# Rounded weights by a casting DMA on Pool's queue instead of copies on ACT, in a hybrid attention block on one core

## The chip, the cores and the metric

The kernel runs as one program on one core of a Trainium2 chip. A core has a matrix engine (TensorE, PE in the profile, with its weight loads shown apart as PEld), a vector engine (DVE), an activation engine (ACT), a general engine (GpSimd, POOL) and a queue engine (SP) that here only issues DMAs. Every engine works through its own list of instructions in order and waits on semaphores for the others. Sixteen DMA engines move data between the main memory and the core's buffer memory; a DMA is issued from the queue of SP, ACT or POOL.

The metric is the device time of one execution in microseconds, the median of three runs.

## The reference

The reference is a decoder block for 512 tokens of width 1024, in float32, with 16 meta tokens put in front (528 rows):

```
h = layer_norm(concat(meta, x))
proj = h @ w_in                       # w_in is 1024 x 10240: ten projections of 1024 columns
q_d,k_d,v_d,g_d, q_s,k_s,v_s,g_s, m_d,m_s = split(proj)
y_d = softmax attention with ALiBi, 8 heads of two 64-wide halves: p0 - lam * p1, then RMS norm per head
y_s = stick-breaking attention, 16 heads of 64 (a reversed running product of sigmoids)
br_d = (y_d * silu(g_d)) @ w_br_diff ;  br_s = (y_s * silu(g_s)) @ w_br_sb
merged = sigmoid(m_d + b0) * br_d + sigmoid(m_s + b1) * br_s
out = layer_norm(2**0.25 * h + merged @ w_out)[16:]
```

## The kernel before

**Products in three parts.** The matrix engine is fed with a rounded 32-bit type (`F32R`). To keep float32 accuracy every operand is split into a rounded part and the rest: `hTh` and `hTl` hold the normalised input, transposed, and each weight tile `raw` becomes `wh` (rounded) and `wl = raw - wh`. A product is then three matmuls: `wh` with `hTh`, `wh` with `hTl`, `wl` with `hTh`.

**Weights.** A weight is a block of 128 output columns, loaded as a tile of 128 partitions x 8 x 128 (512 KB). The list `seq` holds 96 of them in the order in which they are used: 80 blocks of `w_in` and 8 each of the two branch matrices. Weight number n has three tiles, `raw`, `wh` and `wl`, and each kind has three buffers in rotation. `load` (L83) issues the loads of `raw` on SP's queue, `hi` (L91) makes `wh` by a copy on ACT (L97), half a tile at a time, and `lo` (L99) makes `wl` by a subtraction on DVE (L103), half a tile at a time. `prep(n, half)` (L105) calls the three of them; it is called by the projection two places earlier, once when it starts and once half way.

**Projections.** `proj_tok` (L350) is one block for the 512 tokens: 8 slices of three matmuls of 128x512 (L356, L357, L358), 24 in all. `proj_pos` (L363) is one block for all 528 rows, as two halves of 264: 48 matmuls (L370).

**Stages.** After a start (normalisation, the first two query blocks, the first key and value blocks) come 16 units: eight heads of the softmax branch ("d") and eight pairs of heads of the stick-breaking branch ("s"). While the scores of one unit are worked out, the projections of the next are woven in: three weights per d unit (key, value, query), five per s unit (two gates more). Scores are matmuls (L495, L501) whose results DVE and ACT work on (L508, L579, L583, L589, L590 for d; L639, L642, L643, L645, L646 for s); PE then turns them (L514, L519), ACT and DVE split them (L524, L525), and PE multiplies them with the values. POOL does small parts: the ALiBi bias of a head (L563), the low part of the squares (L612), the gating of a result (L388). The late stage (from L720) makes the two branch products and the merge gates, 128x512 projections one after another, and POOL adds the two branches (L740); a tail multiplies with `w_out` and normalises.

**Order.** The statements are not run in the order of the code. From the start on, the framework's scheduler places every instruction on its engine by a timeline of its own, so a change in what an instruction is or where it runs moves the others. The chip then keeps that order on each engine: an instruction that waits holds everything behind it on its engine.

Of the kernel before, what the change touches and what calls it, by code (L numbers as in the profile page):

```python
# [10 lines left out]
F32R = mybir.dt.float32r  # L11
# [5 lines left out]
P = 128  # L17
D = 1024
KT = D // P
# [13 lines left out]
COL = dict(qd=0, kd=1024, vd=2048, gd=3072, qs=4096, ks=5120, vs=6144, gs=7168, md=8192, ms=9216)  # L33
# [10 lines left out]
def hybrid_block_kernel(ctx: ExitStack, tc: tile.TileContext, x, meta, emb_g, emb_b, w_in, b_gate,  # L44
                        diff_lambda, subln_g, w_br_d, w_br_s, w_out, ln_g, ln_b, out):
    nc = tc.nc
    v, s, g, pe = nc.vector, nc.scalar, nc.gpsimd, nc.tensor

    w_in = w_in[0].rearrange("(k p) n -> p k n", p=P)
    w_br_d = w_br_d[0].rearrange("(k p) n -> p k n", p=P)  # L50
    w_br_s = w_br_s[0].rearrange("(k p) n -> p k n", p=P)
# [4 lines left out]
    wpool = ctx.enter_context(tc.tile_pool(name="w", bufs=3))  # L56
# [11 lines left out]
    seq = [("qd", 0), ("qd", 1), ("kd", 0), ("vd", 0)]  # L68
# [11 lines left out]
    raws, split = [], []  # L80
    AHEAD = 2

    def load(n):  # L83
        while len(raws) < min(n, len(seq)):
            kind, i = seq[len(raws)]
            src, c = {"bd": (w_br_d, i * P), "bs": (w_br_s, i * P)}.get(kind) or (w_in, COL[kind] + i * P)
            raw = wpool.tile([P, KT, P], F32, tag="raw", name="raw", bufs=3)
            nc.sync.dma_start(raw, src[:, :, c:c + P])
            raws.append(raw)

    def hi(n, half):  # L91

        if half == 0:
            assert len(split) == n
            split.append([wpool.tile([P, KT, P], F32R, tag=w, name=w) for w in ("wh", "wl")])
        o = ts(half, 4)
        s.copy(split[n][0][:, o, :], raws[n][:, o, :])  # L97

    def lo(n, half, eng=v):  # L99

        o = ts(half, 4)
        wh, wl = split[n]
        eng.tensor_tensor(wl[:, o, :], raws[n][:, o, :], wh[:, o, :].bitcast(F32), op=ALU.subtract)  # L103

    def prep(n, half):  # L105

        load(n + 2)
        if n < len(seq):
            hi(n, half)
            lo(n, half)  # L110

    state = {"n": 0}

# [19 lines left out]
    for o in (ts(0, 512), ts(1, 512)):  # L133
        nc.sync.dma_start(xts[0][:, o], x[0, ts(0, P), o])
    nc.sync.dma_start(xts[1], x[0, ts(1, P), :])
    load(2)
    nc.sync.dma_start(xts[2], x[0, ts(2, P), :])
    nc.sync.dma_start(xts[3], x[0, ts(3, P), :])
    nc.sync.dma_start(mt, meta)
    load(3)  # L140
    nc.sync.dma_start(rows2[0:16], b_gate[0].rearrange("a (k p) -> (a k) p", p=P))
    nc.sync.dma_start(rows2[16:17], subln_g)
# [207 lines left out]
    def proj_tok(res, kind, i, hh=hTh, hl=hTl, o=M):  # L350
        n, wh, wl = weights(kind, i)
        ps = pj.tile([P, 512], F32, tag="pj", name="ps")
        for k in range(KT):
            if k == 0 or k == 4:
                prep(n + AHEAD, k // 4)
            pe.matmul(ps, wh[:, k, :], hh[:, k, o:], start=(k == 0), stop=False)  # L356
            pe.matmul(ps, wh[:, k, :], hl[:, k, o:], start=False, stop=False)  # L357
            pe.matmul(ps, wl[:, k, :], hh[:, k, o:], start=False, stop=(k == KT - 1))  # L358
            if k < KT - 1:
                yield 0.64  # L360
        res.append(ps)

    def proj_pos(res, kind, i):  # L363
        n, wh, wl = weights(kind, i)
        for c in range(2):
            ps = pj.tile([P, 512], F32, tag="pj", name="ps")
            prep(n + AHEAD, c)
            for k in range(KT):
                for m, (a, b) in enumerate(((wh, hTh), (wh, hTl), (wl, hTh))):
                    pe.matmul(ps[:, :H2], a[:, k, :], b[:, k, ts(c, H2)], start=(k == 0 and m == 0),  # L370
                              stop=(k == KT - 1 and m == 2))
                if k < KT - 1:
                    yield 0.33
            res.append(ps)
            if c == 0:
                yield 0.33
# [36 lines left out]
    with tc.tile_pool(name="att", bufs=1) as ap:  # L413
# [259 lines left out]
        for n in range(2):  # L673
            units[n]["A"] = A0[n]
        prep(3, 0)
        prep(3, 1)
        run(keys_values(units[0], *UNITS[0]))
# [82 lines left out]
    for c in range(2):  # L760
        for k in range(0, KT, 2):
            raw = wpool.tile([P, 2, 512], F32, tag="raw", name="rawo", bufs=3)
# [6 lines left out]
    for t in range(NB):  # L769
# [4 lines left out]
        for o, w in parts:  # L774
            c, r = o // 512, ds(o % 512, w)
            ps = pj.tile([P, 512], F32, tag="pj", name="pso")[:, :w]
            for k in range(KT):
                mh, ml = MH[:, k, ts(t, P)], ML[:, k, ts(t, P)]
                wh, wl = WO[c][0][:, k, r], WO[c][1][:, k, r]
# [4 lines left out]
            w = 256 if last else 512  # L784
# [55 lines left out]
```

## Time and profile before

| | |
|---|---|
| time, median of 3 runs | 752.0 us (751.91 to 752.81) |
| the profiled execution's own time | 751.83 us |
| its span, first to last instruction | 750.1 us |
| mean granted clock of the matrix engine | 0.993 |
| PE busy / weight loads busy | 733.0 us (98%) / 651.4 us (87%) |
| DVE busy | 543.7 us (72%) |
| ACT busy | 413.2 us (55%) |
| POOL busy | 85.2 us (11%) |
| moved by DMA | 63.90 MB, 85 GB/s in the mean |

The span is shorter than the time by 1.7 us, which lie before the first and after the last instruction. "Busy" for an engine means that some instruction of it is under way; a wait in front of an instruction is idle time, which the views put down to the instruction that ended it. The busy time of PE overlaps between neighbouring matmuls: a 128x512 matmul is shown with 393 ns, but the next one starts earlier than that. In the rows of a timeline the columns are the start, the duration, engine, line, operation, what is written and read, the shape, and in brackets the idle time before it with what ended it.

### The profile page before, as it was taken

Reading aid. Unit: us, or ns where it says so; the run is one execution under the profiler, and the core shown is the slowest. Engines: PE = TensorE matmul, PEld = TensorE weight load, DVE = VectorE, ACT = ScalarE, POOL = GpSimd, SP = SyncE. Lnnn points to the kernel's source line nnn. Section 1 sums busy time; section 2 is a strip of 40 time slices with the busy share of each in tenths; the row PEclk is TensorE's granted clock in tenths of the full one; section 3 lists DMA queues with packets and bytes.
Section 4 is the critical chain, followed back from the end, with each engine's and each line's share of the span. In section 5 each row is a group of like instructions: output and inputs, shape, how many; then the busy total and the mean of one; then the engine's idle time right before and its main releaser. Section 6 shows DMA issues by size and latency. Waiting matters only on the chain.

```text
span 750.1 us, 11849 instructions
## 1 busy us (share of the span) xinstructions
PE 733.0 (98%) x4390; PEld 651.4 (87%) x4390; DVE 543.7 (72%) x1181; ACT 413.2 (55%) x983; POOL 85.2 (11%) x106
## 2 busy tenths in 40 slices
PE   7999999999999999999999999999999999999996
PEld 6899999999999979898989898988878888888885
DVE  6888898888887789695969596967478343335555
ACT  6476777676777787575647474746473232324200
POOL 5510110111000000000000000001001000000101
PEclk8999999999999999999999999999999999999998
DMA  8132112121212121212222222122244333325221
GB/s 260 32 114 85 57 57 85 57 81 51 68 57 86 56 85 39 75 57 85 57 84 58 84 57 85 57 86 57 84 168 142 110 87 102 95 85 195 86 85 57
DMA packets 105340, 63.90 MB, mean 85 GB/s; under 512 B 2065, under 2 KB 100530, under 8 KB 105282
## 3 DMA queue, kind: packets, MB, share of 16 engines
q1 hardware_dynamic: 104098, 58.93, 26.6%
q10 hardware_dynamic: 1184, 4.20, 1.6%
q8 instruction: 35, 0.57, 0.3%
q14 instruction: 23, 0.19, 0.1%
HBM read 61.03 MB, written 2.10 MB: 84 GB/s over the span
## 4 chain that ended last, share of the span: by engine, by line
PE 90%; DVE 5%; ACT 3%; DMA 1%; issue 1%; POOL 0%; SPq 0%; DVEq 0%; ACTq 0%; POOLq 0%
PE ps L370 23%; PE ps L357 14%; PE ps L358 14%; PE ps L356 14%; PE sc L501 5%; PE t L514 3%; PE pso L782 2%; PE pso L781 2%; PE pso L780 2%; PE t L519 1%; PE av L659 1%; DMA raw<-in_w_in_dram 1%; PE tv L471 1%; PE av L655 1%; DVE hTl L239 1%
## 5 line engine op out<-in xcount | busy, mean ns | idle before, releaser
L103 DVE TENSOR_TENSOR wl<-raw,wh 128x512 fp32r<-128x512 f32 x187 | 131.5, 732 | 63.5 <-ACT wh L97 63.3
L97 ACT CAST wh<-raw 128x512 fp32r<-128x512 f32 x192 | 109.8, 621 | 120.8 <-PE ps L357 111.0
L370 PE MATMUL ps<-hTh,wh 128*128 128x264 f32 x512 | 147.5, 288 | 0.5 <-ACT k L452 0.4
L370 PE MATMUL ps<-hTl,wh 128*128 128x264 f32 x512 | 146.4, 286 | 0.0
L370 PE MATMUL ps<-hTh,wl 128*128 128x264 f32 x512 | 146.3, 286 | 0.0
L356 PE MATMUL ps<-hTh,wh 128*128 128x512 f32 x368 | 144.7, 393 | 0.0
L357 PE MATMUL ps<-hTl,wh 128*128 128x512 f32 x368 | 144.4, 392 | 0.0
L358 PE MATMUL ps<-hTh,wl 128*128 128x512 f32 x368 | 144.3, 393 | 0.0
L370 PEld LDWEIGHTS ps<-hTh,wh 128*128 128x128 f32 x512 | 96.5, 188 | 2.6 <-ACT k L452 0.9
L370 PEld LDWEIGHTS ps<-hTl,wh 128*128 128x128 f32 x512 | 96.6, 189 | 1.1
L370 PEld LDWEIGHTS ps<-hTh,wl 128*128 128x128 f32 x512 | 96.5, 188 | 0.0
L358 PEld LDWEIGHTS ps<-hTh,wl 128*128 128x128 f32 x368 | 69.1, 188 | 13.9
L357 PEld LDWEIGHTS ps<-hTl,wh 128*128 128x128 f32 x368 | 69.2, 188 | 13.2
L356 PEld LDWEIGHTS ps<-hTh,wh 128*128 128x128 f32 x368 | 69.2, 188 | 13.0
L645 DVE TENSOR_TENSOR_SCAN om<-om 128x528 f32<-128x528 f32 (+2 forms) x64 | 55.1, 868 | 9.9 <-ACT om L642 9.1
L501 PE MATMUL sc<-k,A 128*128 128x264 f32 (+2 forms) x256 | 54.1, 305 | 0.0
L525 DVE TENSOR_TENSOR al<-t,ah 128x512 fp32r<-128x512 f32 (+2 forms) x72 | 39.7, 571 | 19.5 <-PE av L661 12.2
L524 ACT CAST ah<-t 128x512 fp32r<-128x512 f32 (+2 forms) x72 | 34.8, 504 | 17.1 <-PE t L514 16.6
L642 ACT ACTIVATE om<-sc 128x264 f32<-128x264 f32 (+3 forms) x80 | 31.7, 397 | 21.1 <-DVE sc L639 20.2
L501 PEld LDWEIGHTS sc<-k,A 128*128 128x128 f32 x256 | 39.7, 189 | 2.5
L514 PE MATMUL t<-ident,apad 128*128 128x128 f32 x240 | 40.9, 272 | 0.7 <-DVE apad L646 0.7
L583 ACT ACTIVATE e<-e,mn 128x528 f32<-128x528 f32 (+3 forms) x64 | 37.0, 578 | 8.1 <-DVE mn L579 7.6
(210 smaller groups left out, 1340.3 us busy)
## 6 DMA issues: line engine op xcount, KB each, us to landing
raw<-in_w_in_dram SPq DMA_DIRECT2D x80, 512.0 KB, 3.8
raw<-in_w_br_diff_dram SPq DMA_DIRECT2D x8, 512.0 KB, 3.7
raw<-in_w_br_sb_dram SPq DMA_DIRECT2D x8, 512.0 KB, 3.8
rawo<-in_w_out_dram SPq DMA_DIRECT2D x8, 512.0 KB, 3.5
hr<-in_x_dram ACTq DMA_DIRECT2D x4, 512.0 KB, 6.8
out_dram<-hr SPq DMA_DIRECT2D x8, 256.0 KB, 2.0
xt<-in_x_dram SPq DMA_DIRECT2D x3, 512.0 KB, 8.8
xt<-in_x_dram SPq DMA_DIRECT2D x2, 256.0 KB, 3.4
```

The source lines that it names most:

```text
L97: s.copy(split[n][0][:, o, :], raws[n][:, o, :])
L103: eng.tensor_tensor(wl[:, o, :], raws[n][:, o, :], wh[:, o, :].bitcast(F32), op=ALU.subtract)
L356: pe.matmul(ps, wh[:, k, :], hh[:, k, o:], start=(k == 0), stop=False)
L357: pe.matmul(ps, wh[:, k, :], hl[:, k, o:], start=False, stop=False)
L358: pe.matmul(ps, wl[:, k, :], hh[:, k, o:], start=False, stop=(k == KT - 1))
L370: pe.matmul(ps[:, :H2], a[:, k, :], b[:, k, ts(c, H2)], start=(k == 0 and m == 0), stop=(k == KT - 1 and m == 2))
L501: pe.matmul(ps[:, :n], q, K[:, m, k0:k0 + n], start=(m == 0), stop=(m == 1))
L514: pe.transpose(t[:, o:o + P], a[:, AOFF[i] + j * P:AOFF[i] + (j + 1) * P], ident)
L524: s.copy(h, t[:, :w])
L525: v.tensor_tensor(l, t[:, :w], h.bitcast(F32), op=ALU.subtract)
L583: s.activation(e[c], e[c], AF.Exp, scale=-1.0, bias=m[:, 0:1], accum_out=zs[:, i, c:c + 1])
L645: v.tensor_tensor_scan(rev, rev, rev, 1.0, ALU.mult, ALU.min)
```

## The change

From the fifth weight on (n of 4 and more, 92 of the 96 weights) `wh` is no longer copied from `raw` on ACT. It is loaded from memory a second time, by a DMA on POOL's queue whose destination has the rounded type, so that the DMA converts on the way. `raw` is still loaded on SP's queue, since `wl = raw - wh` needs it. The subtraction on DVE stays, with both halves called at the second of the two `prep` calls; the DMA is called at the first.

```diff
+    def source(n):
+        kind, i = seq[n]
+        src, c = {"bd": (w_br_d, i * P), "bs": (w_br_s, i * P)}.get(kind) or (w_in, COL[kind] + i * P)
+        return src[:, :, c:c + P]
+
     def load(n):
         while len(raws) < min(n, len(seq)):
-            kind, i = seq[len(raws)]
-            src, c = {"bd": (w_br_d, i * P), "bs": (w_br_s, i * P)}.get(kind) or (w_in, COL[kind] + i * P)
             raw = wpool.tile([P, KT, P], F32, tag="raw", name="raw", bufs=3)
-            nc.sync.dma_start(raw, src[:, :, c:c + P])
+            nc.sync.dma_start(raw, source(len(raws)))
             raws.append(raw)
+
+    def hi_dma(n):
+
+        assert len(split) == n
+        split.append([wpool.tile([P, KT, P], F32R, tag=w, name=w) for w in ("wh", "wl")])
+        g.dma_start(split[n][0], source(n))
...
     def prep(n, half):
 
         load(n + 2)
-        if n < len(seq):
+        if n < len(seq) and n < 4:
             hi(n, half)
             lo(n, half)
+        elif n < len(seq):
+            if half == 0:
+                hi_dma(n)
+            else:
+                lo(n, 0)
+                lo(n, 1)
```

The new function moves the lines below it: L103 of before is L112 of the change, and every line from L121 on has 15 more. The scheduler also moves instructions; three places show it. Numbers after a name tell one tile from another, and the brackets name the semaphores that a row waits for: those that begin with DMAHW count loads on SP's and ACT's queues, those that begin with DMASW the new DMAs of POOL's queue.

The first place is DVE's list in the d stage, at the two subtractions for weight 13, a key block. `sc` is the bank of a score matmul, `e0` and `e1` the scores of the two halves of a head, `V1` the low part of the values. Before:

```order
L590 SCALAR_TENSOR_TENSOR apad0_496<-e1_1307,rz_1310,e0_1306 128x528 [waits DVE_49]
L103 TENSOR_TENSOR wl_1444<-raw_1295,wh_1443 128x512 [waits DMAHW0_49,PE_49,Activation_49]
L103 TENSOR_TENSOR wl_1444<-raw_1295,wh_1443 128x512 [waits Activation_49]
L451 TENSOR_TENSOR k0_1292<-ps_1378,k0_1292 64x264 [waits Activation_49]
L587 RECIPROCAL rz_1310<-zs_1309 128x2 [waits Activation_49]
```

The same weight in the change:

```order
L594 ISA e0_1297,mn_1299<-sc_1388,bias_1295 128x400 [waits PE_49]
L594 ISA mn_1299 128x1
L493 TENSOR_TENSOR V1_1318<-tv_1312,V0_1317 128x384 [waits Activation_49]
L112 TENSOR_TENSOR wl_1435<-raw_1287,wh_1434 128x512 [waits DMAHW0_49,DMASW1_49]
L112 TENSOR_TENSOR wl_1435<-raw_1287,wh_1434 128x512
L594 ISA e1_1298,mn_1299<-sc_1399,bias_1295 128x400 [waits PE_49]
```

The pair now waits for the DMA of POOL's queue and not for ACT, and it stands later: behind the scores from `sc_1388`, ahead of those from `sc_1399`.

The second place is POOL's list in the s stage, where it had only the gating of the results. Before:

```order
L388 TENSOR_TENSOR ydT_491<-sg_4060,ydT_491 128x512 [waits DVE_49]
L388 TENSOR_TENSOR ysT_492<-sg_4097,ysT_492 128x512 [waits DVE_49]
L388 TENSOR_TENSOR ydT_491<-sg_4494,ydT_491 128x512 [waits DVE_49]
L388 TENSOR_TENSOR ysT_492<-sg_4531,ysT_492 128x512 [waits DVE_49]
L388 TENSOR_TENSOR ydT_491<-sg_4928,ydT_491 128x512 [waits DVE_49]
```

In the change:

```order
L403 TENSOR_TENSOR ydT_491<-sg_4025,ydT_491 128x512 [waits DVE_49]
L98 DMA wh_4070<-in_w_in_dram 128x8x128 [waits DMASW1_49,PE_49]
L403 TENSOR_TENSOR ysT_492<-sg_4061,ysT_492 128x512 [waits DVE_49]
L98 DMA wh_4214<-in_w_in_dram 128x8x128 [waits DMASW2_49,PE_49]
L98 DMA wh_4342<-in_w_in_dram 128x8x128 [waits DMASW3_49,PE_49]
L98 DMA wh_4413<-in_w_in_dram 128x8x128 [waits DMASW4_49,PE_49]
L98 DMA wh_4461<-in_w_in_dram 128x8x128 [waits DMASW5_49,DVE_49,PE_49]
```

Five DMAs per unit stand between the gatings, each waiting for PE to be done with the `wh` whose buffer it fills.

The third place is PE's list where the s stage hands over to the late stage. `ghd`, `ghs`, `gls` are the split branch inputs. Before, weight 70 (`wh_6679`) is read for the last time here, and the next weight that fills its buffer, `wh_6785`, is first read 46 rows later:

```order
L356 MATMUL ps_6817<-hTh_143,wh_6748 128x512 [waits Activation_49]
L357 MATMUL ps_6817<-hTl_144,wh_6748 128x512
L357 MATMUL ps_6745<-gls_6622,wh_6679 128x512 [waits DVE_49]
L358 MATMUL ps_6745<-ghs_6621,wl_6680 128x512
L358 MATMUL ps_6782<-hTh_143,wl_6715 128x512 [waits DVE_49]
L356 MATMUL ps_6782<-hTh_143,wh_6714 128x512
```

In the change `wh_6716` takes the buffer of `wh_6647`. The first row here is the one right behind the last read of `wh_6647`, and the last row is the first read of `wh_6716`; between the third and the fourth row six more of the product with `wh_6613` are left out:

```order
L373 MATMUL ps_6713<-hTh_143,wl_6648 128x512
L372 MATMUL ps_6677<-gls_6557,wh_6613 128x512 [waits DVE_49]
L373 MATMUL ps_6677<-ghs_6556,wl_6614 128x512
...
L371 MATMUL ps_6747<-hTh_143,wh_6680 128x512 [waits DMASW4_49,Activation_49]
L372 MATMUL ps_6747<-hTl_144,wh_6680 128x512
L371 MATMUL ps_6781<-ghd_6538,wh_6716 128x512 [waits DMASW5_49,DVE_49]
```

The order has shrunk that distance to 11 rows.

## The prediction

> **What bounds the kernel now.** I read the engine totals first, then the chain that ended last, then busy time by stage.
>
> ```profile
> PE 733.0 (98%) x4390; PEld 651.4 (87%) x4390; DVE 543.7 (72%) x1181; ACT 413.2 (55%) x983; POOL 85.2 (11%) x106
> PE 90%; DVE 5%; ACT 3%; DMA 1%; issue 1%; POOL 0%; SPq 0%; DVEq 0%; ACTq 0%; POOLq 0%
> 33.00:46.00 13.00, 12.63 (x102) 12.24 (x101) 10.22 (x27) 6.77 (x18) 4.69 (x12) 1.00 0.34 97
> 46.00:238.00 192.00, 191.90 (x1359) 181.59 (x1359) 164.59 (x494) 140.26 (x357) 20.41 (x17) 1.00 0.25 71
> 238.00:545.00 307.00, 305.09 (x1879) 270.71 (x1878) 235.60 (x466) 190.24 (x476) 22.13 (x20) 1.00 0.24 69
> 545.00:700.00 155.00, 154.38 (x683) 127.35 (x682) 80.55 (x104) 56.88 (x95) 13.15 (x9) 1.00 0.40 122
> ```
>
> The stretches are the end of the start, the d stage, the s stage and the late stage; the columns are length, then busy time of PE, weight loads, DVE, ACT and POOL, the granted clock, and the DMA share. PE is the bound: from 46 to 700 us it is idle for 0.10 + 1.91 + 0.62 = 2.6 us. So no unloading of ACT can bring more than 2.6 us there, and ACT has only 3% of the chain. DVE is the next one, at 86% in the d stage and 77% in the s stage.
>
> How long a stage's unit is, from rows of the chain that return once per d unit (24.33 us) and once per two s units (75.81 us, so 37.9):
>
> ```profile
> 153.30 3.52 PE ps L370 x29
> 177.63 2.44 PE ps L370 x20
> 327.36 3.52 PE ps L370 x29
> 403.17 3.52 PE ps L370 x29
> ```
>
> The d stage thus has 192 / 24.33 = 7.9 units, the s stage 307 / 37.9 = 8.1. DVE is idle for (192 − 164.59) / 7.9 = 3.5 us per d unit and (307 − 235.60) / 8.1 = 8.8 us per s unit.
>
> **What is removed.** 184 of these copies:
>
> ```profile
> L97 ACT CAST wh<-raw x192: 602/620/678, 8.8 to 683.8; 128x512 fp32r<-128x512 f32 x192
> ACT wh L97 <- PE ps L357: 111.0, 44, 4.3
> DVE wl L103 <- ACT wh L97: 13.3, 8, 1.9
> DVE wl L103 <- ACT wh L97: 22.5, 13, 2.9
> ```
>
> That is 184 x 0.62 = 114 us of ACT, and the 111 us in which ACT stood before a copy until PE freed the buffer. The last two rows are DVE's waits for the copy, in the d and the s stage. All this lies beside PE's work; it is worth 0 to 2.6 us of time, and I take 0.
>
> **What is added: a landing.** Before, a copy starts when PE frees the buffer, and the subtraction soon after:
>
> ```profile
> 148.86 1.14 ACT L97 CAST wh<-raw 128x512 fp32r<-128x512 f32 x2 [0.42 <-PE ps L370]
> 157.59 1.14 ACT L97 CAST wh<-raw 128x512 fp32r<-128x512 f32 x2 [0.48 <-PE ps L370]
> 150.10 1.28 DVE L103 TENSOR_TENSOR wl<-raw,wh 128x512 fp32r<-128x512 f32 x2
> 159.07 0.68 DVE L103 TENSOR_TENSOR wl<-raw,wh 128x512 fp32r<-128x512 f32 x1
> ```
>
> From the freed buffer to the subtraction it is 1.2 and 1.5 us. Afterwards a DMA of 512 KB from POOL's queue stands in between. The trace has none from that queue, so I bound its landing L, issue to landing, by the load of the same bytes from SP:
>
> ```profile
> DMA to landing us min/median/max: 3.5/3.8/7.9
> raw<-in_w_in_dram SPq DMA_DIRECT2D x80, 512.0 KB, 3.8
> q1 hardware_dynamic: 104098, 58.93, 26.6%
> L612 POOL TENSOR_TENSOR sql<-sq,sqh 128x512 fp32r<-128x512 f32 x8 | 10.3, 1291 | 124.3 <-ACT sqh L611 124.3
> ```
>
> The low end is the median load, 3.8 us; the high end the longest, 7.9. About 104098 x 0.52 / 58.93 = 920 packets make one load, so POOL has many pieces to describe, and its nearest rows are far from free: 1.3 us for a pass over half a tile, 2.6 for a whole one. 3.8 plus most of that gives 5.9, the middle of the two ends, which I take. A second copy of the weights doubles SP's queue from 26.6% of the DMA engines to some 50%, which leaves room.
>
> **Where that landing is waited for.** DVE keeps its order. Counting PE rows between the last read of a buffer and the last PE result that DVE needs ahead of the subtraction, at these spacings,
>
> ```profile
> 44.86 0.28 PE L370 MATMUL ps<-hTl,wh 128*128 128x264 f32 x1
> 44.98 0.28 PE L370 MATMUL ps<-hTh,wl 128*128 128x264 f32 x1
> 556.86 0.39 PE L357 MATMUL ps<-gld,wh 128*128 128x512 f32 x1
> 557.09 0.39 PE L358 MATMUL ps<-ghd,wl 128*128 128x512 f32 x1
> ```
>
> (0.12 and 0.23 us per row), the new order puts it 2.1 us after the release in the mean of 23 weights of the d stage and 1.8 us for 38 of the s stage; before, the means were −1.7 and −1.4. For weight 13, shown with the change, `sc_1388` is done 3.2 us after the release. DVE's own rows then take 1 to 2 us more, so DVE stands before the subtraction some 4.0 us after the release and waits L − 4.0. Behind it wait the scores that empty PE's two score banks, and PE's next score matmul, with the projection rows behind that.
>
> - d stage: three weights per unit wait 3 x 1.9 = 5.7 us. DVE's 3.5 us of idle time absorb between half and all of themselves (part of it ends with ACT or PE, whatever DVE does); the middle is 2.6. So 3.1 us per unit, 25 us.
> - s stage: 5 x 1.9 = 9.5 us, less 6.6 (the middle of 4.4 and 8.8): 2.9 per unit, 23 us.
> - Late stage: a buffer is free for two projections, 48 rows of 0.23, 11 us. L plus two subtractions of 0.7 (the 0.68 us row above) is 7.3 us: hidden by those two projections, 0. That cover is gone at L = 9.6.
> - Hand-over to the late stage: `wh_6716` is read 11 rows (2.5 us) after its buffer is free, so PE waits 5.9 − 2.5 = 3.4 us; weight 71 needs its low part 20 rows (4.5 us) after its release, so 5.9 + 0.7 − 4.5 = 2.1. Together 5.5 us.
> - Start: POOL reaches the first new DMA behind the fills of L418 and L423,
>
> ```profile
> 37.37 0.35 POOL L423 MEMSET v<- 128x128 f32 x2
> 42.83 0.39 PE L370 MATMUL ps<-hTh,wh 128*128 128x264 f32 x1 [0.37 <-ACT k L452]
> 45.82 0.64 PE L501 MATMUL sc<-k,A 128*128 128x264 f32 x4
> ```
>
>   so it lands at 37.7 + 5.9 = 43.6, DVE subtracts until 45.0, and only then makes the second half of the keys, which the scores at 45.8 need: about 2 us (0 at L = 3.8, 4 at 7.9).
> - POOL's gating rows and its DMAs queue in the order in which PE ends the projections, so neither holds the other for long; `raw` on SP waits on later subtractions, but is a whole projection ahead. Both 0.
>
> Sum: 25 + 23 + 5.5 + 2 = 55.5 us. The profiled execution took 751.83 us, 1.7 over its span, 0.2 under the median; so 752 + 55 = 807 us. At L = 3.8 only the hand-over is left, 1.3 us: 753. At L = 7.9 the waits are 3.9 each: (11.7 − 2.6) x 7.9 + (19.5 − 6.6) x 8.1 + 9.5 + 4 = 190, 942 us.
>
> **Rivals.**
>
> Hidden landing: L is 4.0 or less, DVE finds the tile there, and ACT's relief gives back up to 2.6 us: 752 + 1.3 − 2.6 = 750.7 to 753.3, not slower by what a measurement can tell (0.2%, 1.5 us). For it: SP's 3.8. Against it: it leaves POOL nothing for its part. It decides at L = 4.0. [...]
>
> POOL too slow: describing the pieces takes longer than PE takes per weight, L of 8 and more. PE uses a weight every 24 x 0.23 = 5.5 us in the late stage and 7.6 to 8.1 before it. At 9.5 us per weight the s unit becomes 5 x 9.5 + 2 x 1.3 = 50 us (+99 in all), the d unit 3 x 9.5 + 2 x 1.3 = 31 (+54), and 25 weights of the late stage 4 us more each (+100): about 1005 us. For it: 920 packets against POOL's slow passes; against it: nothing in the trace shows POOL describing anything.
>
> A lock between DVE and POOL: while POOL ran L612 from 154.53 on, a copy on DVE took 1.00 us where its median is 0.29.
>
> ```profile
> 154.53 1.30 POOL L612 TENSOR_TENSOR sql<-sq,sqh 128x512 fp32r<-128x512 f32 x1 [17.69 <-ACT sqh L611]
> 154.98 1.00 DVE L453 CAST k<-k 64x264 fp32r<-64x264 f32 x1
> L453 DVE CAST k<-k x64: 291/293/1046, 41.1 to 483.4; 64x264 fp32r<-64x264 f32 x64
> ```
>
> If writing a DMA's description does the same once per weight, 64 weights of the d and s stages cost 0.7 us more each: 807 + 45 = 852. [...]
>
> That the DMA moves the bits without rounding would change `wl`, not the time.
>
> **How the numbers follow.** Main case 0.55, POOL too slow 0.20, the lock 0.10, hidden landing 0.15. Of the last, 0.08 lie within 0.2%, 0.04 below (ACT's relief a little larger, or no wait at the hand-over) and 0.03 above: faster 0.04, same 0.08, slower 0.88. The range runs from the hidden landing, 752, to the main case with the long landing, about 950, and leaves out a part of the slow POOL.
>
> **What would show it.** DVE's waits before L112 would be put down to the DMA into `wh`, 2 us each; PE would show gaps before score matmuls in both attention stages and one of 3 us at the hand-over; the late stage would stay 155 us long; ACT would be busy 300 us. I am wrong if the landing from POOL is under 4 us, or if PE's gaps lie in the late stage, where POOL would be the bound.

## The result, and the profile after

The changed kernel takes 765.1 us (median of four runs, 761.7 to 766.7) against 751.95: slower by 1.66%, 95% interval 1.51% to 1.81%. The forecast was 807 us in a range of 752 to 950. The direction and the range held; of the 55 us that the forecast added, 13 came. The execution whose profile is read below took 763.91 us, 12.1 more than the profiled one of before, so the rows account for 12 of the 13.

Engine totals and the chain of the changed kernel, from its page:

```profile
PE 737.8 (97%) x4390; PEld 652.6 (86%) x4390; DVE 537.4 (71%) x1181; ACT 315.6 (41%) x799; POOL 163.8 (21%) x198
PE 61%; DVE 17%; DMA 12%; issue 5%; ACT 3%; POOL 1%; SPq 0%; DVEq 0%; POOLq 0%; ACTq 0%
```

ACT lost 98 us of work and POOL gained 79. The chain now runs through DVE and DMA for 29% of a span of 762.1 us, which is 221 us; the span grew by 12.0. A share of the chain tells where the last releaser stood at each step, not what it cost.

The three long stages of the changed kernel, in the columns of before:

```profile
46.00:238.00 192.00, 191.32 (x1347) 180.20 (x1346) 162.22 (x490) 111.64 (x304) 40.37 (x41) 1.00 0.62 136
238.00:545.00 307.00, 304.62 (x1875) 269.49 (x1874) 234.69 (x466) 148.15 (x394) 57.22 (x60) 1.00 0.65 137
545.00:700.00 155.00, 150.19 (x658) 123.38 (x657) 66.15 (x96) 23.25 (x39) 33.00 (x33) 0.99 0.87 195
```

PE has hardly more idle time in the attention stages than before: 0.7 + 2.4 us, where it was 0.1 + 1.9. It has 4.8 us in the window of the late stage, where it had 0.6. DVE is idle for 29.8 and 72.3 us in the attention stages, where it was idle for 27.4 and 71.4.

PE's waits of the changed kernel from 33 to 545 us, all of them:

```profile
PE ps L385 <- ACT k L467: 2.4, 5, 0.7
PE sc L516 <- DVE mn L594: 0.2, 1, 0.2
PE t L534 <- DVE al L540: 0.2, 1, 0.2
PE ms L633 <- DVE v L502: 0.2, 1, 0.2
```

Before there were three, 2.3 us together. The forecast had put its gaps before score matmuls (`sc`): one of 0.2 us is there. The largest group is projections that wait for ACT's `k`.

To see where the time went, I took the start of each 128x512 projection matmul from both timelines, paired them in order, and subtracted (us, after less before, by the time of before). The rows e1 to e11 belong to the experiments of the next section.

```
at (before)        60   260   544   551   557   568   573   693   709   end
after             0.4   2.1   3.6   5.1   5.5   5.5   9.6   9.6  12.0  11.9
e1 attention      0.4   4.1   4.5   6.8   6.8   6.8   6.8   6.8   6.8   6.8
e2 late          -0.4  -0.4  -0.4   1.2   4.4   4.4   4.4   4.4   5.1   5.1
e3 70-74 by ACT  -0.5   2.6   3.1   5.4   5.4   5.4   5.4   5.4   6.5   6.5
e6 ACT from 62    0.9   3.3   4.6   6.8   8.6   8.6   8.6   8.6   8.6   8.6
e7 idle only      0.9   0.9   1.0   2.0   1.7   1.8   1.8   2.5   2.6   2.6
e10 two halves    1.1  10.1   9.4   9.9  10.0  10.0  10.0  10.0  10.5  10.5
e11 raw twice     0.1   0.1   0.2   0.2   0.1   0.1   0.1   0.1   0.1   0.1
```

(A single entry inside a stage can be off by 2 to 4 us, where the scheduler put that projection elsewhere in the unit; the column 260 is such a place.) The change costs 3.6 us up to the end of the attention stages, 1.9 where the first branch product begins, 4.1 at weight 73, nothing in the late stage, 2.4 at its end.

PE's waits of the changed kernel from 540 us on, all of them:

```profile
PE ps L371 <- DMA wh<-in_w_br_diff_dram: 2.4, 1, 2.4
PE pso L795 <- ACT mh L756: 1.9, 1, 1.9
PE ps L371 <- ACT ghd L743: 1.3, 1, 1.3
PE ps L372 <- DVE gld L744: 1.0, 1, 1.0
```

**The hand-over, first branch product.** The last value product (`av`) ends the attention; from it ACT, DVE, ACT, DVE make the first `ghd` and `gld`, while PE runs what projection rows are left. PE's timeline before:

```profile
547.91 0.39 PE L661 MATMUL av<-al,V 128*128 128x512 f32 x1
...
550.67 0.39 PE L356 MATMUL ps<-ghd,wh 128*128 128x512 f32 x1
551.68 0.50 PE L357 MATMUL ps<-gld,wh 128*128 128x512 f32 x1 [0.62 <-DVE gld L729]
```

And after:

```profile
552.63 0.39 PE L676 MATMUL av<-al,V 128*128 128x512 f32 x1
...
555.75 0.49 PE L371 MATMUL ps<-ghd,wh 128*128 128x512 f32 x1 [1.34 <-ACT ghd L743]
557.27 0.50 PE L372 MATMUL ps<-gld,wh 128*128 128x512 f32 x1 [1.02 <-DVE gld L744]
```

Before, 11 projection rows of 0.23 us lie between; after, 6, since the scheduler put the rest ahead of the last values. The way from the last value to `ghd` is 2.76 us before and 3.12 after. The waits grow from 0.62 to 2.36 us, 1.74 of the 1.9.

**Weight 73.** PE's timeline of the changed kernel where weight 73 (the first `ghd` row here) is first read:

```profile
573.71 0.39 PE L372 MATMUL ps<-hTl,wh 128*128 128x512 f32 x1
576.54 0.77 PE L371 MATMUL ps<-ghd,wh 128*128 128x512 f32 x1 [2.45 <-DMA wh<-in_w_br_diff_dram]
577.11 0.63 PE L372 MATMUL ps<-gld,wh 128*128 128x512 f32 x1
...
579.64 0.40 PE L372 MATMUL ps<-hTl,wh 128*128 128x512 f32 x1
```

The landing shows as 2.45 us of wait. But the seven rows behind it start 0.40 to 0.57 us apart, where 0.23 is usual: 3.10 us from 576.54 to 579.64, 1.5 more than seven rows take. Wait and slow rows together are the 4.0 of the 4.1 us.

### The profile page after: what moved, and what is told of

It reads as the page before. It is cut to its first block, busy times and chain, and to the rows that moved or that the text cites. A ratio compares the mean times of both kernels' runs of the same rounds, so it can differ in the third digit from the quotient of the medians.

```text
span 762.1 us, 11819 instructions
## 1 busy us (share of the span) xinstructions
PE 737.8 (97%) x4390; PEld 652.6 (86%) x4390; DVE 537.4 (71%) x1181; ACT 315.6 (41%) x799; POOL 163.8 (21%) x198
## 3 DMA queue, kind: packets, MB, share of 16 engines
q0 software_dynamic: 95680, 48.24, 35.9%
q1 hardware_dynamic: 104098, 58.93, 27.6%
## 4 chain that ended last, share of the span: by engine, by line
PE 61%; DVE 17%; DMA 12%; issue 5%; ACT 3%; POOL 1%; SPq 0%; DVEq 0%; POOLq 0%; ACTq 0%
PE ps L371 12%; PE ps L373 12%; PE ps L372 12%; PE ps L385 10%; DMA wh<-in_w_in_dram 7%; DVE wl L112 4%; PE t L529 3%; PE sc L516 2%; DMA rawo<-in_w_out_dram 2%; PE pso L797 2%; PE pso L795 2%; PE pso L796 2%; DVE e L594 1%; DVE k L466 1%; DVE om L660 1%
## 5 line engine op out<-in xcount | busy, mean ns | idle before, releaser
L112 DVE TENSOR_TENSOR wl<-raw,wh 128x512 fp32r<-128x512 f32 x187 | 127.8, 722 | 134.6 <-DMA wh<-in_w_in_dram 66.1
L98 POOL DMA_DIRECT2D wh<-in_w_in_dram x76 | 68.7, 904 | 317.0 <-PE ps L373 145.3
L660 DVE TENSOR_TENSOR_SCAN om<-om 128x528 f32<-128x528 f32 (+2 forms) x64 | 53.4, 858 | 3.9 <-ACT om L657 3.4
L516 PE MATMUL sc<-k,A 128*128 128x264 f32 (+2 forms) x256 | 55.9, 309 | 0.2 <-DVE mn L594 0.2
```

The source lines that it names most:

```text
L98: g.dma_start(split[n][0], source(n))
L516: pe.matmul(ps[:, :n], q, K[:, m, k0:k0 + n], start=(m == 0), stop=(m == 1))
L660: v.tensor_tensor_scan(rev, rev, rev, 1.0, ALU.mult, ALU.min)
```

## The experiments

Each is the changed kernel or the one before with one edit, and with the order that the scheduler then makes of it. They are called e1, e2, e3, e5, e8, e4, e11, e6, e10 and e7, in the order below. The first four ran beside the kernel before at 751.6 us, the others at 752.1.

### Only the attention weights

```diff
-        if n < len(seq) and n < 4:
+        if n < len(seq) and not 4 <= n < 69:
```

> The casting DMA feeds weights 4 to 68 (the two attention stages) and ACT copies feed the late stage as before. Theory A (the landing is absorbed while a freed buffer is not read again for 13 us or more, and the loss of 13 us sits at three places around the hand-over and the tail): the 3.6 us that the changed kernel had lost by the end of the s stage, and the 1.9 us at the first branch product, since ACT still has the merge gate ahead of it there; no gap at weight 73 and no late tail. 752 + 3.6 + 1.9 = 757.5 us. Theory B (every new landing costs alike, 13.1 / 92 = 0.14 us per weight): 752 + 65 x 0.14 = 761 us.

757.9 us (755.5 to 759.4), ratio 1.0080 (1.0058 to 1.0102): near the 757.5 of theory A, and theory B's 761 lies above the interval. The delay is 4.5 us at the end of the attention stages, 6.8 after the first branch product, and flat from there: weight 73 and the tail cost nothing when ACT copies from 69 on.

### Only the late weights

```diff
-        if n < len(seq) and n < 4:
+        if n < len(seq) and n < 69:
```

> The complement: ACT copies up to weight 68, the casting DMA for weights 69 to 95. The order now leaves 6.8 us or more between the last read of a buffer and its next first read at weights 71 to 74 (2.5 to 6.1 in the changed kernel). Theory A: no loss up to the hand-over, at most 1 us there, and the 2.4 us of the tail if it comes from the late subtractions: 752 to 755.5 us. Theory B: 752 + 27 x 0.14 = 755.8 us, lost evenly over the late stage.

756.1 us (755.2 to 757.1), ratio 1.0056 (1.0039 to 1.0072). Both theories had numbers near it, so the time decides nothing; its trace does. There is no wait at weight 73, whose buffer is free 6.8 us of PE rows ahead here (2.5 in the changed kernel). The tail costs 0.7 us and not 2.4, though all late weights come by the casting DMA. The other 4.8 us of the 5.5 are lost at the first branch product, on PE's timeline:

```profile
551.85 0.50 PE L371 MATMUL ps<-ghd,wh 128*128 128x512 f32 x1 [1.38 <-ACT ghd L743]
553.31 0.79 PE L372 MATMUL ps<-gld,wh 128*128 128x512 f32 x1 [0.96 <-DVE gld L744]
...
559.02 0.61 PE L373 MATMUL ps<-ghd,wl 128*128 128x512 f32 x1
559.45 0.42 PE L371 MATMUL ps<-ghd,wh 128*128 128x512 f32 x1
```

and by a window of e2 (the last columns are the granted clock, the DMA share and GB/s):

```profile
555.00:560.00 5.00, 5.00 (x14) 3.84 (x14) 4.62 (x9) 5.00 (x10) 0.00 (x0) 0.55 1.08 362
```

After 2.3 us of waits PE's rows start 0.43 us apart for 6 us, and the granted clock is 0.55. The waits grow by 1.7 us against before, and the 14 rows from 553.31 to 559.45 take 3.0 us more than they would at 0.23: 4.7 of the 4.8 us by which the delay rises.

### The five weights of the hand-over by ACT

```diff
-        if n < len(seq) and n < 4:
+        if n < len(seq) and (n < 4 or 70 <= n <= 74):
```

> The changed kernel with ACT copies for weights 70 to 74 alone. Theory A: the 4.1 us at weight 73 are gone, the 3.6 us before it, the 1.9 us at the first branch product and the 2.4 us of the tail stay: 761 us. Theory B: five landings fewer, 0.7 us: 764.4 us.

760.95 us (758.6 to 763.6), ratio 1.0125 (1.0099 to 1.0151), where theory A said 761. On the trace the 4.1 us of weight 73 are gone, 2.3 at the first branch product stay, and 1.1 at the tail. The agreement with 761 is partly luck: the profiled execution was the fastest of the four, 758.6 us, and its rows show a delay of 6.5 us, so that the other 2 to 3 us of the median are in no row that was read.

### Every casting DMA issued twice

```diff
         g.dma_start(split[n][0], source(n))
+        g.dma_start(split[n][0], source(n))
```

on top of e1.

> As the run with the casting DMA in the attention stages alone, but each of those DMAs is issued twice into the same tile, the second after the first has landed: a landing of about 10.8 us in place of 5.4. Theory A: 10.8 and 1.4 us for the subtractions are under the 13 to 18 us for which a buffer is free, so little is added, 0 to 10 us over the run with one DMA: 757 to 768 us. Theory B, in the prediction's form (DVE waits for the landing less 4 us at every weight, less what its idle time absorbs): 3 x 6.8 - 2.6 us per d unit and 5 x 6.8 - 6.6 per s unit, 140 + 220 us: about 1110 us.

831.5 us (823.6 to 834.2), ratio 1.1046 (1.0987 to 1.1104). Neither theory: far more than slack that takes up everything, far less than every microsecond of landing on PE. The second issue waits for the first to land (both write one tile; POOL waits for it at 47 of the 65, 224 us in all), so from the first issue to the last landing it is 11.7 us in the median (6.4 between the issues, 5.5 to land). The delay rises through both attention stages to 81.5 us. Of DVE's and PE's waits from 33 to 600 us:

```profile
DVE wl L113 <- DMA wh<-in_w_in_dram: 121.7, 46, 5.9
```

```profile
PE t L535 <- DVE al L541: 16.8, 12, 2.6
PE av L671 <- ACT af L569: 12.4, 7, 3.5
PE ps L386 <- DMA wh<-in_w_in_dram: 4.8, 4, 2.4
```

The landing does reach PE, mostly by way of DVE's splits (`al`) standing late behind the subtraction, directly or through ACT's `af`, which waits for them for 128 us in the same stretch, and less by the weight itself.

### Half of each weight sent ahead once more

```diff
+        g.dma_start(split[n][0][:, 0:4, :], source(n)[:, 0:4, :])
         g.dma_start(split[n][0], source(n))
```

on top of e1.

> The change for weights 4 to 68, with half of each weight's bytes sent once more ahead of it on the same queue: the landing goes from 5.4 us to about 8.1, between the change (5.4) and the doubled landing (11.1). Theory A (DVE's and PE's spare time takes up the landing until it is used up, somewhere between 8 and 11 us): 758 to 770 us. Theory B (the cost is proportional to the landing beyond 5.4: 73.7 us for 5.7 us more): 790 to 795 us. Theory C (the forecast's rule, each weight's wait behind 4.0 us comes to lie on PE): about 940 us.

797.3 us (796.8 to 800.3), ratio 1.0612 (1.0590 to 1.0635). My landing for it was wrong: the two DMAs land one after the other here too, 10.0 us from the first issue in the median (4.6 between the issues, 5.5 to land) instead of 8.1. So the time near theory B's number does not show a straight line. With the measured landings the cost in the attention stages (delay at 544 us, 65 weights) is

```
landing us      5.4    10.0   11.7
delay us        4.5    39.2   81.5
us per weight   0.07   0.60   1.25
```

It bends: little at 5.4, and 1.25 - 0.60 = 0.65 us more per weight for the last 1.7. If the landing alone did it, the spare time is used up somewhere between 5.4 and 10.0. In both runs POOL also stood waiting between the two issues, and the scheduler, which knew of the second DMA, put the subtractions later, so this is a dose of landing, POOL's queue and order together.

### The traffic alone, on POOL

```diff
+            if 4 <= n < 56 and half == 0:
+                kind, i = seq[n]
+                spare = ysT[:, 6:8, :].bitcast(F32R).rearrange("p a (b n) -> p (a b) n", n=P)
+                g.dma_start(spare, w_in[:, :, ds(COL[kind] + i * P, P)])
             hi(n, half)
```

in the kernel before.

> Weights 4 to 55 are still copied by ACT as in the kernel before; besides, POOL starts the same casting DMA for each of them, into a stretch of SBUF that nobody reads yet, so that the second read of the weights and POOL's part in it are there and nobody waits for a landing. Theory A (the loss in the attention stages comes from waiting for the landing, the traffic itself is free): 751 to 753 us, and the same matmuls start within 1 us of the kernel before at the end of the attention stages. Theory B (the doubled traffic, or POOL being busy beside DVE, makes the loss): 754 to 756 us, since 52 of the 65 weights would bring 0.8 of the 4.5 us that the change of the attention weights alone had lost by there.

807.6 us (803.3 to 808.4), ratio 1.0725 (1.0695 to 1.0755): neither theory. Without a reader the DMAs were not tied to anything; POOL ran ahead and had started all 52 by 302 us. They share one destination, so each waits on POOL's queue for the one before to land. POOL's own piece of the softmax branch, the low part of the squares, stands behind them. POOL's and PE's waits from 33 to 545 us:

```profile
POOL ysT L112 <- DMA ysT<-in_w_in_dram: 182.9, 48, 5.9
```

```profile
PE ms L623 <- POOL sql L616: 34.1, 8, 7.5
```

The run says nothing on traffic. It shows what one engine's queue can do: a DMA that waits holds the arithmetic behind it, and PE then waited 34 us for POOL. The eight d units lost 44 us in all; the granted clock there was 0.94, where it was 1.00 before. In the changed kernel each DMA waits for PE to free a buffer, and no wait of PE for POOL is in its trace from 33 us on.

### The traffic alone, on SP

```diff
+            if 4 <= len(raws) < 69:
+                nc.sync.dma_start(raw, src[:, :, c:c + P])
             nc.sync.dma_start(raw, src[:, :, c:c + P])
```

in the kernel before.

> The kernel before, with weights 4 to 68 read twice by SP's queue into the same raw tile, the second after the first: the bytes moved from HBM in the attention stages are those of the change for these weights, ACT still copies, POOL starts nothing, and no weight is waited for on POOL's queue. Theory A (traffic costs nothing, the 3.6 to 4.5 us of the attention stages come from the landing that DVE waits for): 751 to 753 us and a delay under 1 us at 545 us. Theory B (the traffic makes them): 755 to 757 us. If ACT or DVE wait for raw in many places, the run says nothing on either.

752.5 us (751.6 to 753.0), ratio 1.0007 (0.9997 to 1.0016), and a delay of 0.2 us at 544. Its DMA issues, and DVE's longest group of waits from 33 to 545 us:

```profile
raw<-in_w_in_dram SPq DMA_DIRECT2D x145, 512.0 KB, 3.8
```

```profile
DVE wl L105 <- ACT wh L99: 36.3, 22, 2.9
```

65 more loads land as fast as the others, and DVE waits for ACT as before. Reading the weights twice costs nothing here, at 142 and 133 GB/s in the two attention stages, where the changed kernel moves 136 and 137. (The DMAs here are SP's and don't convert.) That leaves the wait for the landing, POOL's part and the new order for the 3.6 us; no run takes the three apart.

### ACT from weight 62 on

```diff
-        if n < len(seq) and n < 4:
+        if n < len(seq) and not 4 <= n < 62:
```

> The casting DMA only for weights 4 to 61; ACT copies the last eight weights of the attention stages and all later ones as in the kernel before, so that ACT and DVE have the old order when the branch products begin. Theory A (the 2 us at the first branch product come from the order of ACT and DVE around the last attention weights): the delay against the kernel before stays at 2.5 to 4.5 us from the end of the attention stages to the end, 754 to 756 us. Theory B (they come from the delay gathered before, or from DVE being late on the whole): it grows by another 2 us at the first branch products as with the change for 4 to 68, 757 to 759 us.

760.0 us (759.4 to 760.5), ratio 1.0103 (1.0088 to 1.0118). It loses the 2 us and more, and theory A as I wrote it is wrong: ACT's order at that point is that of before, and that does not help. PE's timeline shows why:

```profile
555.01 0.39 PE L676 MATMUL av<-al,V 128*128 128x512 f32 x1
557.50 0.50 PE L371 MATMUL ps<-ghd,wh 128*128 128x512 f32 x1 [2.10 <-ACT ghd L743]
558.75 0.50 PE L372 MATMUL ps<-gld,wh 128*128 128x512 f32 x1 [0.75 <-DVE gld L744]
```

Not one projection row is left between the last value and `ghd`. PE's order sets most of this wait, not ACT's: with 11 or 12 rows of cover (before, e10) the two waits are 0.6 and 1.1 us, with 6 or 7 (after, e1, e2, e3) 2.3 to 2.7, with none (e6 here, e4, e8) 2.75 to 2.9. The rest is the way from the last value to `ghd`, which is between 2.5 (e6) and 3.9 us (e1, e3). The delay rises by 2.2 us there, and by another 1.8 in eight rows at 0.43 us behind it.

### In two halves

```diff
-        g.dma_start(split[n][0], source(n))
+        for o in (ts(0, 4), ts(1, 4)):
+            g.dma_start(split[n][0][:, o, :], source(n)[:, o, :])
```

> The changed kernel with each casting DMA cut into two of 256 KB, so that the subtraction of the first half can begin when that half has landed; in the earlier run of half a weight such a DMA landed in 3.9 us where the whole one takes 5.4. In the order that comes out, PE has 12 projection rows between the last value products and the first branch product (6 in the changed kernel, 11 before), and weight 73's buffer is released 6.4 us ahead of its first use (2.5). Theory A (the 6 us lost at the hand-over are the missing rows of cover and the short reuse of weight 73's buffer): the delay against the kernel before stays within 1 us from the end of the attention stages to the start of the w_out products, no wait for a casting DMA there, and with 2 to 4 us in the attention stages and up to 2.4 at the tail 755 to 759 us. Theory B (it comes from DVE or the traffic being late there, whatever the order): again 5 to 6 us at the hand-over, 761 to 765 us.

762.9 us (762.2 to 762.9), ratio 1.0144 (1.0129 to 1.0159). All waits of PE from 545 us to the end:

```profile
PE ps L373 <- DVE gld L745: 0.8, 1, 0.8
PE ps L372 <- ACT ghd L744: 0.3, 1, 0.3
```

With 12 rows of cover and 6.4 us for weight 73's buffer the hand-over costs 0.6 us and the tail 0.5, although every late weight still comes by the casting DMA. That is theory A on the hand-over. (The halves of the branch matrices also land sooner, in 3.8 to 4.6 us where whole ones take 4.8, but 6.4 us covers either.) The attention stages did the opposite of what I expected: 9.4 us, where the whole DMA costs 3.6, and that alone puts the time into theory B's range. The halves land in 4.3 us, but POOL starts twice as many (busy 218 us, 164 with whole ones). Whether the order or POOL makes the 6 us more was not tried.

### A wait without the traffic

```diff
+        if n == "d":
+            spare = lp.tile([P, 3, 480], mybir.dt.bfloat16, name="spare")
+            s.copy(spare, ydT[:, 0:3, 0:480])
         for j in range(8):
```

ahead of the `ghd` copies in the kernel before.

> The kernel before, with one ACT copy of 1440 elements (about 1.5 us) into a tile that nobody reads, ahead of the first ghd: PE's wait for the first branch product grows from 0.6 us to about 2, with no second read of any weight. Theory A (after a wait of this size the granted clock falls for some us, and that costs as much again): 13 or so matmuls then start 0.43 us apart where 0.23 is usual, the delay is 3 to 4.5 us, 754.5 to 756 us. Theory B (the slow spacing comes with the full DMA queues of that moment, which this kernel does not have): spacing 0.23, a delay of 1 to 1.5 us, 752.5 to 753.2 us.

753.85 us (752.9 to 754.5), ratio 1.0024 (1.0014 to 1.0034). The added copy took 1.39 us, but PE's wait grew only to 1.09 us (0.87 for `ghd`, 0.22 for `gld`), not to 2. No slow rows follow. The wait was too short to tell the two theories of the slow rows apart. Two other traces speak against theory B. In the kernel before, the DMA queues are full at that moment and the clock is whole:

```profile
555.00:560.00 5.00, 5.00 (x23) 4.14 (x23) 4.97 (x9) 5.00 (x11) 0.00 (x0) 1.00 1.00 351
```

In e6 the slow rows come with a DMA share of 0.67:

```profile
559.00:563.00 4.00, 4.00 (x12) 3.09 (x12) 4.00 (x8) 4.00 (x9) 0.00 (x0) 0.57 0.67 218
```

So full queues neither suffice nor are needed. What decides which wait is followed by slow rows stays open.

## Why the prediction was wrong

**The landing: right.** I took 5.9 us between 3.8 and 7.9. The DMA issues of the changed kernel:

```profile
raw<-in_w_in_dram SPq DMA_DIRECT2D x80, 512.0 KB, 4.0
wh<-in_w_in_dram POOLq DMA_DIRECT2D x76, 512.0 KB, 5.4
wh<-in_w_br_diff_dram POOLq DMA_DIRECT2D x8, 512.0 KB, 4.8
```

That is 1.4 us over SP's load of `w_in`. The share of the DMA engines, forecast at some 50%, came to 27.6 + 35.9 = 64%. The hidden landing, which decided at 4.0, fell with the measured 5.4. What it said of the attention stages came close all the same: at 5.4 us little was lost there.

**POOL too slow: wrong. The lock: slow copies are there, but rare.** POOL is held 0.88 us per DMA, by all instructions of that line:

```profile
L98 POOL DMA_DIRECT2D wh<-in_w_in_dram x76: 876/876/1107, 38.1 to 670.7; - x76
```

That is a tenth of the 9.5 us that this rival was sized with. A DMA of 256 KB, with 528 packets in place of 1040, holds POOL for 0.75 us (the median of 65 in e8): some 0.1 us less for half the pieces. That describing them is what POOL does in that time was my assumption; the runs show the time alone. The subtraction did not become slower in the changed kernel, 722 ns in the mean, 732 before. But the lock had been read from another row, DVE's copy of `k`, and that row shows it. On DVE:

```profile
174.25 0.70 DVE L468 CAST k<-k 64x264 fp32r<-64x264 f32 x1
```

And on POOL:

```profile
173.98 0.88 POOL L98 DMA_DIRECT2D wh<-in_w_in_dram  x1 [8.17 <-PE ps L385]
```

The copy begins while POOL works on the DMA, ends 0.1 us after it and takes 0.70 us, where the median of the 64 copies is 0.29. Of the others beside such a DMA and nothing else on POOL, two took 0.63 and 0.40 and four kept their 0.29: 0.9 us in all, where the rival had counted 0.7 for each of 64 weights. The copies together lost 1.3 us in the changed kernel and 5.5 before, there beside POOL's arithmetic.

**The two attention terms, 25 + 23 us: this is the step that failed.** They measured 1.7 and 1.5. "DVE stands before the subtraction and waits" is right, and DVE's waits of the changed kernel show it. In the d stage:

```profile
DVE wl L112 <- DMA wh<-in_w_in_dram: 16.0, 11, 3.5
```

In the s stage:

```profile
DVE wl L112 <- DMA wh<-in_w_in_dram: 30.6, 21, 3.8
DVE wl L112 <- issue: 10.3, 4, 3.0
DVE wl L112 <- PE ps L372: 4.5, 1, 4.5
```

16 + 45 us, where 1.9 us for each weight made 45 + 77. (The five waits put down to issue and to PE end within 0.1 us of a landing too.) Two thirds of the weights in the s stage and half in the d stage wait at all; the others find the tile there. The 1.9 us at every weight is the term that was mis-sized. I had DVE stand before the subtraction 4.0 us after the release; from the start of the DMA on POOL it comes there after 5.1 us in the mean of the d stage and 4.6 in the s stage, anywhere between 1.3 and 7.3, and the landing takes 5.1 and 5.5 us in the mean, not 5.9. With the measured waits, 2.0 us per d unit and 5.6 per s unit, my own middles for what DVE's idle time absorbs, 2.6 and 6.6, leave nothing.

What I set against the wait was the smaller error. Idle time that absorbs all of itself and not "between half and all" would still have left (5.7 − 3.5) x 7.9 + (9.5 − 8.8) x 8.1 = 23 us of the 48. It fits the measured waits better: 2.0 of 3.5 us per d unit and 5.6 of 8.8 per s unit went in, and PE lost 3.2 in both stages together (the split into 1.7 and 1.5 is less certain). Part of that idle time had been DVE's wait for the ACT copy at the same instruction, 13.3 + 22.5 us, which only changed its releaser. Idle time ahead of the subtraction grew by 61 - 36 = 25 us, other waits of DVE shrank by 22, and DVE's idle time in the two stages rose by 2.4 + 0.9 = 3.3 us. Whether the others shrank because DVE came later or because ACT had less to do was not taken apart. The doses fit a limit that a longer landing passes: at 10.0 us of landing the attention stages cost 39 us, at 11.7 they cost 82; but POOL's queue and the order changed with them.

DVE's idle time rose by 3.3 us and PE lost 3.2, so the rows need no further cover on PE's side to explain the small loss. Whether PE has any, from the two banks of scores or the projection rows woven in, I did not measure.

**The hand-over, 5.5 us: 6.0, a near hit that is partly luck.** Weight 73 was forecast with a wait of 3.4 us from the 11 rows; it waited 2.45, and 1.5 us of slow rows came on top. The 2.1 us for weight 71 did not come. In their place came 1.9 us at the first branch product, from cover that the new order took away, which I had not looked at, and the slow rows were in no term. e3 takes away the loss at weight 73 alone, e10 both.

**Start, 2 us: 0.4.** **Late stage, 0: right**, to 0.1 us in every run that has it. DVE waits in it for landings, but two projections cover them, as the working said.

**Tail, not in the forecast: 2.4 us.** I had dismissed `raw` on SP as "a whole projection ahead". A `raw` buffer is now held until the subtraction after the landing, and SP's loads of `w_out` stand behind the last of them in its queue. Before:

```profile
674.59 21.45 SPq L763 DMA_DIRECT2D rawo<-in_w_out_dram  x8
```

After:

```profile
689.40 21.56 SPq L778 DMA_DIRECT2D rawo<-in_w_out_dram  x8
```

14.8 us later, 5.2 more than the delay of 9.6. Their conversions on ACT and DVE then crowd the last `mh`, for which PE waits 1.9 us. e1 and e6, whose late weights are ACT's, have no such loss, and there the loads start no later than the delay. In e2, e3 and e10 the loads start 3.7 to 4.5 us later than the delay, and the tail costs 0.5 to 1.1 us. So late loads and the loss go together, but not in size. That SP's queue is the cause was read from the rows and not tried by itself.

**Nothing to win, right.** ACT lost 98 us of work and PE got nothing for it; e2, which unloads ACT in the late stage alone, gains nothing there. No run was faster than the kernel before, whose PE is idle for 2.6 us from 46 to 700 us.

## What to carry to other kernels

When a change puts a longer way in front of a tile, do not charge the same wait at every use from a mean position: ask at each use whether the consumer comes before the tile or after it. Then set the consumer's old wait for the same tile, and its other idle time, against the sum. Where a scheduler decides the order, count the rows that the last engine has left to run at each point where one stage hands over to the next: 6 rows of cover in place of 11, and a buffer free for only 11 rows, cost 6.0 of the 12 us here; an order that left more of both cost 0.6. And an engine's queue is one line: a DMA that waits in it holds the arithmetic behind it, 34 us of waits in one experiment, whether or not anyone needs its data.

## What was not expected of the hardware

After some short waits the matrix engine runs at half its pace for 3 to 6 us: rows of 128x512 start 0.43 us apart, not 0.23, and the granted clock is 0.55 (e2), 0.57 (e6) and 0.66 (after, e8) in windows of 4 to 5 us there. So a wait can cost much more than the table of waits says: 2.45 became 4.0 us at weight 73, and a rise of 1.7 became 4.7 in e2. It followed waits of 2.34 (e2, two parts), 2.45 (after), 2.85 (e6, two parts) and 2.9 us (e8, two parts); it did not follow 2.36 us (after, first branch product) and 2.66 (e1 and e3), nor 1.1 (e7, e10). The length alone does not decide, and no run shows what does.

A DMA that converts from float32 to the rounded type on POOL's queue landed, in the changed kernel, 1.4 us later than the plain load of the same bytes for `w_in` (5.4 against 4.0 us), though not for the branch matrices (4.8 against 5.0 to 5.2); in e4, with one under way at a time, it took 4.6. It held POOL for 0.88 us. 256 KB of it landed in 4.3 us (e10) and 3.9 (e8): half the bytes save 1.1 to 1.5 us of the 5.4.
